# Issuing the adaLN weight and condition loads from GpSimd's queue in a two-layer diffusion backbone

## The chip, the cores and the metric

The kernel runs on one core of a Trainium2 chip. The metric is the device time of one execution in microseconds (us), the median over repeated executions. The profile is one execution taken by the hardware profiler.

## What is computed

Two layers of a diffusion backbone over 512 latent and 256 context tokens, width 1024, all in float32. Each layer is a half-step SwiGLU, a token mixer (differential attention in layer 0, windowed grouped-query attention in layer 1) and another half-step SwiGLU. Every sub-layer normalises its input and modulates it with shift, scale and gate vectors, which are products of the layer's adaLN matrix with SiLU of a condition:

```python
mod_l = (jax.nn.silu(c) @ ada_w[i] + ada_b[i])[:, None, :]      # 9 vectors of 1024 for latent tokens
mod_c = jax.nn.silu(c_ctx) @ ada_w[i] + ada_b[i]                # and for context tokens
sh1, sc1, g1, sh2, sc2, g2, sh3, sc3, g3 = jnp.split(mod_l, N_MOD, axis=-1)
def ffn_step(t, sh, sc, g, wi, wo):
    return t + 0.5 * g * swiglu(modulate(rms(t), sh, sc), wi, wo)
x = ffn_step(x, sh1, sc1, g1, pre_wi, pre_wo)
x = x + g2 * mixer(modulate(rms(x), sh2, sc2), ...)
x = ffn_step(x, sh3, sc3, g3, post_wi, post_wo)
```

## The kernel before, in words

TensorE (PE) multiplies everything as split float32: each operand is cut in a high part, made by ScalarE (L73), and a low part, made by VectorE (L74), and each product takes three matmuls. A weight slab of 512 KB is loaded into a tile `raw` (three buffers, L97) by a DMA that the sync engine SP issues; the tile is free again when VectorE has made the last low part from it (`wlo`, L74). The up products of a feed-forward use seven products where eight would be plain (L470), with sums of weights made by VectorE (L456 to L459) and sums of results (L479 to L507). The down products (L584) are added to the residual `x` by VectorE (L396).

The adaLN vectors 0 to 2 of layer 0 are made at the start (`vector_job`, L190, and `scale_job`, L205). All the others are made by `Halves`, beside the products of the feed-forwards before they are needed: one step is one load of 128 x 512 values of the adaLN matrix (`wh`, 256 KB, L247, three buffers) and one or two VectorE products with SiLU of the conditions (`ch`, L236 and L237) that sum along the row (L250). Eight steps fill `part`, and GpSimd adds it to the vector (L254); GpSimd also sets each vector to its bias ahead of that (`bias`, L227 and L229). `beside(3)` calls one step in each up block from the fifth on, `between(13)` 13 steps in the 16 tiles of a group of down products, and `oproj` two steps in a tile. There are 240 such loads and 16 of conditions: 80 steps in layer 0's first feed-forward, 16 in the attention's output product, 64 in layer 0's second feed-forward and 80 in layer 1's first.

The order on each engine's queue is set by a planner, when the program is built. It takes instructions as they become ready by its own estimate of their times, the earlier ones in the program's order first, and can move one ahead of others on its engine. `keep` (`tc.keep_in_program_order`) pins an instruction behind the one that the program last gave to the same engine; the loads L236 and L247 are kept, the slab loads L97 mostly are not. So before the change a load of `wh` stands on SP behind the slab load that the program issued last, and after it behind the last instruction that the program gave to GpSimd. Queues run in order: an instruction that waits for a free buffer holds what stands behind it.

GpSimd otherwise does little in the feed-forwards: sums of squares for the next normalisation in the last group of down products (L343), the power -1/2 (L300) and, in the attention, powers and rotary sums.

Of the kernel before, what the change touches and what calls it, by code (L numbers as in the profile page):

```python
# [17 lines left out]
P = 128  # L18
D = 1024
KC = D // P  # L20
# [22 lines left out]
def hybrid_backbone_kernel(ctx: ExitStack, tc: tile.TileContext, I, out):  # L43
    nc = tc.nc
# [25 lines left out]
    keep = tc.keep_in_program_order  # L70
# [143 lines left out]
    class Halves:  # L214
# [6 lines left out]
        def add(self, l, ms):  # L221
            def bias(m):
                md = const.tile([P, 2, KC], F32, name=f"mod{l}_{m}")
                mods[l][m] = md[:, 0], md[:, 1], md
                b = adab[:, l, m * KC:(m + 1) * KC].unsqueeze(1).broadcast_to([P, 2, KC])
                if m in (1, 4, 7):
                    nc.gpsimd.tensor_scalar_add(md, b, 1.0)  # L227
                else:
                    nc.gpsimd.tensor_copy(md, b)  # L229

            def silu(room, q):
                cs = []
                for nm in ("c", "c_ctx"):
                    pool, tag, bufs = (small, "ar", 3) if room[1] == "wh" else room
                    t = pool.tile([P, 512], F32, name="ch", tag=tag, bufs=bufs)
                    keep(nc.sync.dma_start(t, I[nm][q * 512:(q + 1) * 512].partition_broadcast(P)))  # L236
                    nc.scalar.activation(t, t, AF.Silu)  # L237
                    cs.append(t)
                self.c = cs

            def job(room, q, m, d):
                types = (0, 1) if l == 0 or m < 5 else (0,)
                if d == 0:
                    self.part = small.tile([P, 2, KC], F32, name="part", tag="part", bufs=2)
                pool, tag, bufs = room
                w = pool.tile([P, 512], F32, name="wh", tag=tag, bufs=bufs)
                keep(nc.sync.dma_start(w, I["ada_w"][l, m * KC + d, :, q * 512:(q + 1) * 512]))  # L247
                for ty in types:
                    o = w if ty == types[-1] else small.tile([P, 512], BF16, name="junkh", tag="tmp", bufs=4)
                    nc.vector.scalar_tensor_tensor(o, w, 1.0, self.c[ty], ALU.mult, ALU.mult,  # L250
                                                   accum_out=self.part[:, ty, d:d + 1])
                if d == KC - 1:
                    md, n = mods[l][m][2], len(types)
                    nc.gpsimd.tensor_add(md[:, :n], md[:, :n], self.part[:, :n])  # L254
                    if q == 1 and m in (2, 8):
                        nc.gpsimd.tensor_scalar_mul(md[:, :n], md[:, :n], 0.5)

            for q in range(2):
                for m in ms:
                    for d in range(KC):  # L260
                        def f(room, q=q, m=m, d=d):
                            if q == 0 and d == 0:
                                bias(m)
                            if m == ms[0] and d == 0:
                                silu(room, q)
                            job(room, q, m, d)
                        self.steps.append(f)
# [1041 lines left out]
```

## Time and profile before

| | us |
|---|---|
| median of 3 runs | 2820.3 (2819.34 to 2823.11) |
| the profiled execution's own time | 2823.49 |
| its span in the profile | 2821.3 |
| TensorE busy in the span | 2705.1 (96%) |
| VectorE busy | 2176.2 (77%) |
| ScalarE busy | 1205.7 (43%) |
| GpSimd busy | 339.3 (12%) |

Busy time of TensorE is that of its matmuls, which are pipelined. SP has no busy time in the profile, since instructions that issue DMAs are not counted; its waits are shown as those of SPq. In a wait, the engine on the left stood idle until the instruction on the right was done.

### The profile page before, as it was taken

What the parts mean: (1) busy time and instruction counts of PE and PEld (TensorE: products, weight loads), DVE (VectorE), ACT (ScalarE), POOL (GpSimd) and SP (SyncE); (2) the same over time, 40 slices, a digit from 0 to 9 for tenths busy, and PEclk for the clock granted to TensorE, in tenths of its full rate; (3) what the DMA queues carried; (4) which work ended last, traced back from release to release, by engine and by line L of the source; (5) the groups of instructions that cost most, each with busy time, mean ns of one, the idle gap of its engine ahead of it and who ended that gap; (6) DMA issues with size and microseconds to landing.
All of it is one profiled execution on the core that took longest, in us unless ns stands there. A gap on an engine that the chain in (4) does not pass through costs nothing. (4 is left out here: it accounts for less than half of the span.)

```text
span 2821.3 us, 47391 instructions
## 1 busy us (share of the span) xinstructions
PE 2705.1 (96%) x18028; PEld 2565.6 (91%) x18028; DVE 2176.2 (77%) x4703; ACT 1205.7 (43%) x2995; POOL 339.3 (12%) x464
## 2 busy tenths in 40 slices
PE   6899999999999899999999999999999999999999
PEld 4799998899999878999899989999999999999999
DVE  8788887876867768877787697777777766588887
ACT  4433332355656644333233352333235666444443
POOL 1000000034533421000000100000003421100000
PEclk9999999999999999999999999999999999999999
DMA  7234433321101142332333223433332101233232
GB/s 278 82 109 127 138 98 111 107 105 46 31 31 31 42 134 63 120 113 78 116 120 102 63 64 124 135 123 95 124 115 93 46 16 38 68 98 100 96 98 97
DMA packets 97555, 266.48 MB, mean 94 GB/s; under 512 B 12464, under 2 KB 16560, under 8 KB 97200
## 3 DMA queue, kind: packets, MB, share of 16 engines
q1 hardware_dynamic: 90816, 251.78, 27.6%
q10 hardware_dynamic: 6512, 11.68, 1.3%
q8 instruction: 142, 2.33, 0.3%
q14 instruction: 85, 0.70, 0.1%
HBM read 256.07 MB, written 7.34 MB: 93 GB/s over the span
## 5 line engine op out<-in xcount | busy, mean ns | idle before, releaser
L73 ACT CAST whi<-raw 128x512 fp32r<-128x512 f32 x548 | 336.1, 620 | 650.6 <-PE ps_dn L584 291.8
L584 PE MATMUL ps_dn<-ah,whi 128*128 128x256 f32 (+1 forms) x1456 | 464.9, 322 | 11.7 <-DVE x L396 9.5
L584 PE MATMUL ps_dn<-al,whi 128*128 128x256 f32 (+1 forms) x1456 | 462.2, 320 | 0.1
L584 PE MATMUL ps_dn<-ah,wlo 128*128 128x256 f32 (+1 forms) x1456 | 455.1, 319 | 1.1 <-DVE wlo L74 1.0
L74 DVE TENSOR_TENSOR wlo<-raw,whi 128x512 fp32r<-128x512 f32 x548 | 378.2, 695 | 65.5 <-ACT whi L73 49.9
L470 PE MATMUL ps_up<-h_h,whi 128*128 128x384 f32 (+1 forms) x1216 | 394.6, 325 | 8.3 <-DVE u L497 6.3
L470 PE MATMUL ps_up<-h_h,wlo 128*128 128x384 f32 (+1 forms) x1216 | 392.2, 324 | 0.7 <-DVE wlo L74 0.7
L470 PE MATMUL ps_up<-h_l,whi 128*128 128x384 f32 (+1 forms) x1216 | 392.5, 323 | 0.0
L396 DVE SCALAR_TENSOR_TENSOR x<-ps_dn,mod,x 128x256 f32<-128x256 f32 (+1 forms) x442 | 241.0, 556 | 126.6 <-PE ps_dn L584 103.0
L584 PEld LDWEIGHTS ps_dn<-ah,whi 128*128 128x128 f32 x1456 | 276.6, 191 | 35.8 <-ACT whi L73 8.5
L73 ACT CAST whi<-s 128x512 fp32r<-128x512 f32 x304 | 188.3, 620 | 266.6 <-PE ps_up L470 220.4
L584 PEld LDWEIGHTS ps_dn<-ah,wlo 128*128 128x128 f32 x1456 | 276.4, 191 | 21.8 <-DVE wlo L74 2.0
L584 PEld LDWEIGHTS ps_dn<-al,whi 128*128 128x128 f32 x1456 | 277.8, 191 | 19.6 <-DVE al L74 0.3
L470 PEld LDWEIGHTS ps_up<-h_h,whi 128*128 128x128 f32 x1216 | 229.0, 188 | 14.0 <-DVE u L497 8.9
L74 DVE TENSOR_TENSOR wlo<-s,whi 128x512 fp32r<-128x512 f32 x304 | 208.5, 687 | 31.4 <-ACT whi L73 27.7
L470 PEld LDWEIGHTS ps_up<-h_h,wlo 128*128 128x128 f32 x1216 | 228.3, 188 | 2.8 <-DVE wlo L74 2.3
L470 PEld LDWEIGHTS ps_up<-h_l,whi 128*128 128x128 f32 x1216 | 228.9, 188 | 0.5
L254 POOL TENSOR_TENSOR mod<-mod,part 128x16 f32<-128x16 f32 (+1 forms) x30 | 13.2, 439 | 1428.6 <-DVE wh L250 1428.6
L673 PE MATMUL ps_qkv<-whi,h_h 128*128 128x256 f32 x608 | 177.8, 292 | 3.2 <-DVE a L629 2.2
L250 DVE SCALAR_TENSOR_TENSOR wh<-wh,ch 128x512 f32<-128x512 f32 x240 | 163.4, 693 | 18.3 <-DMA wh<-in_ada_w 18.2
L673 PE MATMUL ps_qkv<-wlo,h_h 128*128 128x256 f32 x608 | 174.1, 286 | 0.7 <-DVE wlo L74 0.7
L673 PE MATMUL ps_qkv<-whi,h_l 128*128 128x256 f32 x608 | 173.6, 286 | 0.0
(236 smaller groups left out, 6536.5 us busy)
## 6 DMA issues: line engine op xcount, KB each, us to landing
wh<-in_ada_w SPq DMA_DIRECT2D x240, 256.0 KB, 3.8
raw<-in_pre_wi SPq DMA_DIRECT2D x88, 512.0 KB, 3.5
raw<-in_post_wi SPq DMA_DIRECT2D x88, 512.0 KB, 3.5
raw<-in_pre_wo SPq DMA_DIRECT2D x44, 512.0 KB, 3.6
raw<-in_post_wo SPq DMA_DIRECT2D x44, 512.0 KB, 3.6
araw<-in_ada_w SPq DMA_DIRECT2D x16, 512.0 KB, 4.4
raw<-in_a_w_qk SPq DMA_DIRECT2D x16, 512.0 KB, 3.5
araw<-in_ada_s SPq DMA_DIRECT2D x8, 512.0 KB, 10.0
```

The costliest lines, as they stand in the source:

```text
L73: nc.scalar.copy(hi, src)
L74: nc.vector.tensor_sub(lo, src, hi.bitcast(F32))
L250: nc.vector.scalar_tensor_tensor(o, w, 1.0, self.c[ty], ALU.mult, ALU.mult, accum_out=self.part[:, ty, d:d + 1])
L254: nc.gpsimd.tensor_add(md[:, :n], md[:, :n], self.part[:, :n])
L396: nc.vector.scalar_tensor_tensor(x[:, d, s0:s0 + n], ps, gate[ty][:, d:d + 1], x[:, d, s0:s0 + n], ALU.mult, ALU.add)
L470: nc.tensor.matmul(ps, ww, z[:, k, :n], start=first and k == 0 and i == 0, stop=k == 3 and i == 2, skip_group_check=True)
L584: nc.tensor.matmul(ps, wv, a[:, s0:s0 + n], start=fi == 0 and k == 0, stop=fi == nf - 1 and k == 2)
L673: nc.tensor.matmul(ps, h[:, k, bt], w, start=n == 0, stop=n == 23)
```

## The change

The loads of the condition halves and of the adaLN weight halves are issued by GpSimd instead of SP. Their `keep` stays, and so pins them on the other queue. Nothing else is edited.

```diff
@@ def silu(room, q):
                     t = pool.tile([P, 512], F32, name="ch", tag=tag, bufs=bufs)
-                    keep(nc.sync.dma_start(t, I[nm][q * 512:(q + 1) * 512].partition_broadcast(P)))
+                    keep(nc.gpsimd.dma_start(t, I[nm][q * 512:(q + 1) * 512].partition_broadcast(P)))
                     nc.scalar.activation(t, t, AF.Silu)
@@ def job(room, q, m, d):
                 w = pool.tile([P, 512], F32, name="wh", tag=tag, bufs=bufs)
-                keep(nc.sync.dma_start(w, I["ada_w"][l, m * KC + d, :, q * 512:(q + 1) * 512]))
+                keep(nc.gpsimd.dma_start(w, I["ada_w"][l, m * KC + d, :, q * 512:(q + 1) * 512]))
```

## Rows read from the trace of the kernel before

**Rows 1.** The page: span, and busy time and count of two engines.

```profile
span 2821.3 us, 47391 instructions
PE 2705.1 (96%) x18028; PEld 2565.6 (91%) x18028; DVE 2176.2 (77%) x4703; ACT 1205.7 (43%) x2995; POOL 339.3 (12%) x464
```

**Rows 2.** Stretches: length, busy PE, PEld, DVE, ACT, POOL (instructions), clock, DMA share, GB/s.

```profile
70.00:80.00 10.00, 3.46 (x19) 2.70 (x17) 10.00 (x29) 2.17 (x5) 0.00 (x0) 0.90 0.00 0
...
330.00:564.00 234.00, 225.69 (x1283) 210.59 (x1282) 191.17 (x423) 73.53 (x131) 2.48 (x6) 1.00 0.35 113
...
1130.00:1550.00 420.00, 412.55 (x2334) 390.81 (x2333) 338.03 (x713) 142.50 (x261) 4.11 (x8) 0.99 0.33 108
1690.00:2100.00 410.00, 408.43 (x2316) 386.81 (x2315) 318.00 (x651) 138.53 (x252) 4.91 (x11) 1.00 0.38 122
```

**Rows 3.** Waits, 121 to 564 us: who, for whom; us in total, times, longest.

```profile
DVE junkh L250 <- DMA wh<-in_ada_w: 6.7, 7, 1.8
PE ps_up L470 <- DVE u L497: 3.2, 1, 3.2
PE ps_dn L584 <- DVE x L396: 3.2, 1, 3.2
```

**Rows 4.** Waits, 1090 to 1560 us.

```profile
DVE junkh L250 <- DMA wh<-in_ada_w: 7.3, 7, 1.9
PE ps_dn L584 <- DVE x L396: 5.4, 3, 3.2
```

**Rows 5.** Waits, 1690 to 2110 us.

```profile
DVE wh L250 <- DMA wh<-in_ada_w: 18.2, 18, 2.3
...
PE ps_up L470 <- DVE u L491: 0.4, 1, 0.4
```

**Rows 6.** Waits of PE, 990 to 1130 us (the attention's output product).

```profile
PE ps_dn L750 <- DVE wlo L74: 2.7, 1, 2.7
```

**Rows 7.** DVE in order of time, 330 to 346 us: start, length [idle before].

```profile
334.31 0.69 DVE L250 SCALAR_TENSOR_TENSOR junkh<-wh,ch 128x512 bf16<-128x512 f32 x1 [1.76 <-DMA wh<-in_ada_w]
...
340.71 0.69 DVE L250 SCALAR_TENSOR_TENSOR junkh<-wh,ch 128x512 bf16<-128x512 f32 x1 [1.10 <-DMA wh<-in_ada_w]
```

**Rows 8.** Waits of SP's queue over the whole span.

```profile
SPq L97 <- DVE wlo L74: 1912.3, 261, 46.4
SPq L247 <- DVE wh L250: 130.1, 108, 5.3
```

**Rows 9.** SP's queue in order of time, 260 to 330 us.

```profile
262.35 14.60 SPq L97 DMA_DIRECT2D raw<-in_pre_wi  x2
277.00 1.19 SPq L247 DMA_DIRECT2D wh<-in_ada_w  x1
```

**Rows 10.** SP's queue in order of time, 0 to 135 us.

```profile
120.43 0.42 SPq L236 DMA_DIRECT2D ch<-in_c  x1
```

**Rows 11.** The tile `wh`: durations in ns (min/median/max), starts; DMA to landing.

```profile
L247 SPq DMA_DIRECT2D wh<-in_ada_w x240: 327/422/1867, 121.4 to 2088.2; - x120
L250 DVE SCALAR_TENSOR_TENSOR wh<-wh,ch x240: 675/685/1219, 128.9 to 2092.5; 128x512 f32<-128x512 f32 x120
...
DMA to landing us min/median/max: 2.5/3.8/6.3
```

**Rows 12.** GpSimd in order of time, 0 to 135 us.

```profile
16.44 0.20 POOL L229 COPY mod<-adab 128x16 f32<-128x16 f32 x1 [16.01 <-DMA adab<-in_ada_b]
...
21.69 1.04 POOL L300 TENSOR_TENSOR r<-v,neghalf 128x4 f32<-128x4 f32 x1
22.69 0.19 POOL L229 COPY mod<-adab 128x16 f32<-128x16 f32 x1
26.09 1.21 POOL L300 TENSOR_TENSOR r<-v,neghalf 128x2 f32<-128x2 f32 x1 [3.20 <-DVE v L298]
```

**Rows 13.** The line L229: durations in ns (min/median/max), first and last start.

```profile
L229 POOL COPY mod<-adab x10: 191/266/1198, 16.4 to 22.7; 128x16 f32<-128x16 f32 x10
```

**Rows 14.** DVE in order of time, 0 to 135 us.

```profile
22.76 0.69 DVE L305 TENSOR_TENSOR dg<-ident,r 128x512 f32<-128x512 f32 x1 [1.79 <-POOL r L300]
```

**Rows 15.** Groups on GpSimd, 121 to 564 us: busy, mean ns, idle before.

```profile
L254 POOL TENSOR_TENSOR mod<-mod,part 128x16 f32<-128x16 f32 x10 | 4.3, 432 | 510.4 <-DVE wh L250 510.4
```

## The prediction, as it was put on record

> **What bounds the kernel now.** I read the page's busy times first. TensorE is busy 2705.1 of 2821.3 us [rows 1], so all that any edit of loads can win is the 116 us in which it isn't. Then the stretches in which the moved loads run, three feed-forwards: there it is busy 225.7 of 234, 412.6 of 420 and 408.4 of 410 us [rows 2]. Then who made TensorE wait in them, and whether that one had itself waited for a moved load. In layer 0's first feed-forward VectorE waited 6.7 us for `wh`, and TensorE lost 3.2 us to the residual sum L396 and 3.2 us to L497 [rows 3]; in the second one VectorE waited 7.3 us, and TensorE lost 5.4 us to L396 [rows 4]; in layer 1's, VectorE waited most, 18.2 us, and TensorE lost 0.4 us [rows 5]. Of these stalls the one to L396 in rows 3 has its cause in sight: 2.86 us of waits for `wh` on VectorE [rows 7], shortly ahead of it on the same queue. The reader is to see that late `wh` loads cost VectorE some 32 us, and that at most about 10 of them reach TensorE.
>
> **The change, part by part.** The sum is made against the profiled execution, 2823.5 us (a span of 2821.3 and 2.2 around it); it lies 3.2 us above the median of the runs, and I subtract that at the end.
>
> *SP loses 256 issues.* An issue takes 0.42 us [rows 11], but SP's time is waiting: 1912 us for `raw` buffers, and only 130 us, in 108 waits, at a `wh` load [rows 8]. A slab load behind such a wait comes at most some 1.2 us sooner, with a buffer that is its true limit. Worth 0.
>
> *GpSimd gains 256 issues.* In a feed-forward it works 4.3 of 443 us on L254 [rows 15], so the issues have cover there; what stands behind a load that waits for its tile is L254, for which only later stages wait. The duration of an issue on GpSimd isn't in this trace. From below it is SP's 0.42 us [rows 11], from above the 1.21 us of a small power [rows 12]; I take 1.04 us, the other power, since it is an instruction of the same queue at the place where it counts. 0 in the feed-forwards.
>
> *The start.* Here there is no cover. The planner takes the bias copies L229 as early as it can: all ten, those of layer 1 too, run from 16.4 to 22.7 us [rows 13], though the program has most of them hundreds of us later. The first two `ch` loads will be pinned behind the first of these copies and nothing else; their tile is free from the beginning, so I expect them at about 17 us instead of 120.4 [rows 10]. The power that the first normalisation needs waits on that queue behind the copies until 21.69 us [rows 12], and VectorE waits 1.79 us for it [rows 14]. Two issues ahead of it make it 2 x 1.04 = 2.1 us later, and VectorE, which soon after has no idle time left (10.00 of 10 us busy, with TensorE at 3.5, [rows 2]), passes that on. +2.1 us; ends 0 (the planner puts them behind the power) and 2 x 1.21 = 2.4 us. A gain is excluded, as nothing leaves that queue.
>
> *The pace.* Before, a `wh` load waits behind the slab load ahead of it: two slab loads hold SP from 262.35 to 276.95 us, and the next `wh` goes out at 277.00 [rows 9]. After, it is pinned only behind the biases, long done, or, in a vector's second half, behind the L254 of the vector before. So it goes out as soon as its tile is free, and its sums fill VectorE's idle time from the start of a stage, rather than come in bursts of 13 steps. What this can win is the stalls after late loads: 3.2 us of L396 in rows 3, 5.4 in rows 4, and 2.7 in the output product [rows 6], 11.3 in all; from below 0. I take the two long ones, 3.2 + 3.2 = -6.4 us: the first has late loads ahead of it, the second (the longest in rows 4) I take to have the same cause, and the short ones look like plain crowding of VectorE.
>
> *The landing.* A `wh` lands 3.8 us after issue now, at most 6.3 [rows 11]. How late it lands from GpSimd isn't shown: 0 to 2.5 us later (6.3 - 3.8); I take 1.0, about one GpSimd instruction ahead of the transfer. VectorE waits for `wh` in 7 + 7 + 18 = 32 cases, and TensorE loses 3.2 + 3.2 + 0.4 = 6.8 us (the longest ones) for 32.2 us of those waits, a share of 0.21 [rows 3 to 5]. With deeper prefetch I expect half as many waits at the landing, those after each L254 among them: 16 x 1.0 x 0.21 = +3.4 us; ends 0 and the second rival below.
>
> Sum: 2.1 - 6.4 + 3.4 = -0.9 us, 2822.6 for the profiled execution, 2819.4 for the median: 2819 us, which a measurement of this kernel can't tell from no change (it takes about 0.2%, 5.6 us).
>
> One rule bears on the first step. Rows 8 show a queue that waits for buffers and not for its own issue time. The Trainium skill ("DMA: Bandwidth & Descriptors", section "Issuing engines are not separate DMA queues") says that DMAs from any engine run on the same 16 DMA engines, and that another issuer saves only the sequencer's time. By that rule alone the sum would be 0; it leaves out the order of the queue that the load moves to, which is what my terms come from.
>
> **The rivals.**
>
> *The new pace clears all the crowding (faster).* Every sum is done ahead of need, and no load is waited for: -11.3, with 0 to +2.1 at the start, about -10 us: 2810. For it: in the last stretch VectorE is less full (318 of 410 us, against 338 of 420) and its waits no longer reach TensorE [rows 2, 5]. Against it: the sums will keep VectorE full for longer, and a queue without slack passes on every slip.
>
> *Descriptors held up (slower).* GpSimd's work is held while VectorE runs an instruction with large operands: L229 takes 266 ns as a rule and 1198 at most [rows 13]. If an issue is held so too, `wh` lands up to 2.5 us late, the planner's places for the sums are too early, and each third load is waited for, not each seventh: 80 x 1.0 x 0.21 = +17 us, 2837; with 2.5 us, 80 x 2.5 x 0.21 = +42 us, 2862. It decides once `wh` takes over about 5 us to land and VectorE's waits for it pass some 80 us. Against it: in a feed-forward L254 takes 432 ns in the mean beside a VectorE that is as full [rows 15].
> The skill ("SBUF — State Buffer", section "SBUF: two separate sides") says that such loads starve while VectorE copies or casts in a two-port mode, and "Who interferes with whom" there exempts sums of two tensors. By the first the time would be this rival's; by the second it would not come about. No row of before has such a load.
>
> *It does nothing (same).* The planner keeps the sums where they stand, since VectorE's order is set by its other work; loads come earlier and wait in their tiles: 2820.
>
> **How the numbers follow.** Forecast (2819, terms cancelling) 0.35; nothing happens 0.13; all crowding clears 0.28; descriptors held up 0.24. Faster by over 0.2% (below 2814.7): 0.29, the faster rival and a little of the forecast's own spread. Slower (above 2825.9): 0.25. Within: 0.46. The range starts at 2808 (the largest gains, 2820.3 - 11.3, and 1 us of the runs' spread) and reaches up to 2838, the slower rival at its middle price; beyond lie the held-up loads at their full price.
>
> **What would show it.** Right: `ch` loads at some 17 us on GpSimd's queue and the power after 23 us; `wh` loads ahead of the slab loads beside them; VectorE's waits for `wh` below 32 us; no TensorE stall of 3 us near 343 and 1370 us. Wrong: a landing over 5 us, or new waits of TensorE on VectorE early in each feed-forward, where the sums now crowd; or an order on VectorE in all later stages that differs so much that the stalls of the attention, which no step here touches, move by several us.

## The result, and the profile after

The changed kernel takes 2869.8 us in the median of 4 runs (2865.42 to 2875.09), the kernel before 2821.5 us beside it: a ratio of 1.0166, 95% interval [1.0153, 1.0179]. It is slower by 48 us, where 2819 us and no measurable change were forecast, and the time lies outside the range.

The profiled execution of the changed kernel took 2865.4 us. Its page gives the span, the busy times and, in the last line, the issues of `wh` (count, size, median us from issue to landing); it answers to [rows 1].

```profile
span 2863.6 us, 47501 instructions
...
PE 2712.5 (95%) x18028; PEld 2572.9 (90%) x18028; DVE 2179.2 (76%) x4703; ACT 1205.4 (42%) x2995; POOL 476.8 (17%) x720
...
wh<-in_ada_w POOLq DMA_DIRECT2D x240, 256.0 KB, 3.2
```

The span has grown by 42.3 us, of which TensorE's busy time is only 7.4 (2712.5 less 2705.1): the other 35 us are idle time of TensorE. VectorE does the same work (2179.2 against 2176.2 us). So the work itself hardly became dearer; something now stands in TensorE's way. The same stretches as in [rows 2], after (length, then busy PE, PEld, DVE, ACT, POOL, then clock, DMA share, GB/s):

```profile
1130.00:1550.00 420.00, 396.68 (x2244) 374.90 (x2243) 331.79 (x701) 137.36 (x252) 36.00 (x68) 0.98 0.31 100
...
1690.00:2100.00 410.00, 394.17 (x2222) 371.36 (x2222) 308.65 (x627) 134.69 (x247) 45.18 (x87) 0.99 0.35 113
```

TensorE is idle for 23.3 and 15.8 us there, where it was idle for 7.4 and 1.6. To see which part of the program pays, I cut both traces at the first product of each stage (for a feed-forward, L537 and then L470; for the attention, L673 or L686; for its output, L750). Length of each stage in us, and TensorE's idle time in it:

```
stage                                   before         after        after - before
start                                118.7 / 34.2   117.7 / 33.9       -1.0
layer 0, first feed-forward          480.7 / 11.7   487.7 / 15.8       +7.0
layer 0, attention                   403.9 / 24.7   398.5 / 21.6       -5.4
layer 0, output product               84.2 /  7.3    84.1 /  8.4       -0.1
layer 0, second ff, blocks of L537    55.4 /  1.8    59.5 /  2.7       +4.1
layer 0, second ff, from L470 on     481.5 / 10.1   497.6 / 26.0      +16.1
layer 1, first ff, blocks of L537     60.4 /  3.2    65.4 /  6.1       +5.0
layer 1, first ff, from L470 on      473.3 /  4.3   490.9 / 18.5      +17.6
layer 1, attention                   238.6 /  5.6   238.7 /  5.8       +0.1
rest                                 424.7 / 10.0   423.6 /  9.0       -1.1
```

The three feed-forwards with sums beside them give 49.8 us; the other stages give 7.5 back. Two profiled executions of one and the same kernel (the first experiment below and its repeat) differ by up to 4.2 us in a stage, so the 7.0 of layer 0's first feed-forward and the -5.4 of its attention lie little above the scatter; what is clear of it are layer 0's second feed-forward and layer 1's first. Where the sums went is seen by asking for VectorE's busy time of L250 alone, stretch by stretch, at the start and the end of layer 0's second feed-forward. Before (length, busy us of these instructions and their count, clock, DMA share, GB/s):

```profile
1088.00:1143.00 55.00, 0.00 (x0) 0.97 0.13 42
1143.00:1163.00 20.00, 4.17 (x13) 1.00 0.55 171
1163.00:1203.00 40.00, 11.99 (x36) 1.00 0.34 112
...
1400.00:1640.00 240.00, 32.27 (x96) 0.99 0.29 93
```

After, the same stretches:

```profile
1088.00:1143.00 55.00, 10.11 (x30) 0.91 0.32 103
1143.00:1163.00 20.00, 8.05 (x23) 0.73 0.20 62
1163.00:1203.00 40.00, 19.18 (x59) 0.92 0.53 169
...
1400.00:1640.00 240.00, 0.00 (x0) 1.00 0.20 67
```

Up to 1163 us VectorE now has 18.2 us of sums, where it had 4.2: 14.0 us more. And there was no room for them. All engines in the first of these stretches, before (PE, PEld, DVE, ACT, POOL):

```profile
1088.00:1143.00 55.00, 53.18 (x338) 48.63 (x338) 52.55 (x109) 28.43 (x62) 0.75 (x1) 0.97 0.13 42
```

VectorE was busy for 52.55 of 55 us without a single sum in it. The 14 us more come out at TensorE as one stall. The longest waits after, whole span (who, for whom; us in total, times, longest):

```profile
PE ps_up L470 <- ACT whi L73: 22.2, 6, 14.6
```

VectorE's queue in order of time, at the end of that stall (start, length, idle before; no idle time stands in these lines), then ScalarE's:

```profile
1155.36 0.68 DVE L456 TENSOR_TENSOR s<-raw 128x512 f32<-128x512 f32 x1
1155.96 0.68 DVE L250 SCALAR_TENSOR_TENSOR junkh<-wh,ch 128x512 bf16<-128x512 f32 x1
...
1159.54 0.68 DVE L457 TENSOR_TENSOR s<-s,raw 128x512 f32<-128x512 f32 x1
1160.15 0.68 DVE L250 SCALAR_TENSOR_TENSOR wh<-wh,ch 128x512 f32<-128x512 f32 x1
...
1161.84 0.68 DVE L458 TENSOR_TENSOR s<-raw 128x512 f32<-128x512 f32 x1
1162.44 0.68 DVE L250 SCALAR_TENSOR_TENSOR junkh<-wh,ch 128x512 bf16<-128x512 f32 x1
...
1163.05 0.68 DVE L459 TENSOR_TENSOR s<-raw,s 128x512 f32<-128x512 f32 x1
```

```profile
1163.77 0.62 ACT L73 CAST whi<-s 128x512 fp32r<-128x512 f32 x1 [5.15 <-DVE s L459]
```

This is the whole chain: TensorE needs the high part `whi` of a sum of weights `s`, ScalarE waits 5.15 us for `s`, and the four instructions that make it (L456 to L459) stand on VectorE with sums of adaLN halves between them. VectorE has no idle time during the stall, so it is not waiting for a load there. TensorE's clock pays as well. The same 20 us before and after:

```profile
1150.00:1170.00 20.00, 19.92 (x114) 19.53 (x113) 18.98 (x46) 8.87 (x17) 0.00 (x0) 1.00 0.50 167
```

```profile
1150.00:1170.00 20.00, 5.56 (x20) 5.55 (x21) 19.81 (x50) 5.48 (x11) 4.48 (x9) 0.57 0.36 110
```

With TensorE busy for 5.56 us instead of 19.92, the granted clock of the stretch is 0.57 instead of 1.00, near the lower of its two levels (1.2 of 2.4 GHz); over the whole execution it is 0.981 against 0.988.

The two other feed-forwards differ. Layer 1's first has the same wait once more, with 6.6 us (waits of TensorE after, 1640 to 2180 us):

```profile
PE ps_up L470 <- ACT whi L73: 7.0, 2, 6.6
```

Layer 0's first has no such stall; just ahead of its first L470 VectorE had room. All engines from 98 to 118 us, before and after, where 8.37 us of sums came in:

```profile
98.00:118.00 20.00, 20.00 (x120) 17.57 (x119) 8.74 (x16) 5.94 (x12) 0.00 (x0) 1.00 0.10 36
98.00:118.00 20.00, 20.00 (x123) 17.77 (x122) 18.84 (x47) 7.58 (x16) 4.29 (x8) 1.00 0.39 129
```

TensorE is busy for all of that stretch in both.

Why the sums came to the start of layer 0's second feed-forward is on GpSimd's queue (start, length, idle before):

```profile
1092.61 0.62 POOL L236 DMA_DIRECT2D ch<-in_c  x1 [3.49 <-ACT h_h L380]
1103.23 0.54 POOL L236 DMA_DIRECT2D ch<-in_c_ctx  x1 [10.00 <-ACT h_h L380]
1103.76 1.60 POOL L247 DMA_DIRECT2D wh<-in_ada_w  x3
```

and on SP's before:

```profile
1144.89 0.42 SPq L236 DMA_DIRECT2D ch<-in_c  x1
1145.36 0.42 SPq L236 DMA_DIRECT2D ch<-in_c_ctx  x1
1145.83 0.43 SPq L247 DMA_DIRECT2D wh<-in_ada_w  x1
```

The first weight load of this feed-forward goes out 42 us earlier. Over the whole span the loads ran from 121.4 to 2088.2 us [rows 11]; now they are all out by 1863.4. VectorE's idle time in front of its sums until a load landed (us, times), before:

```profile
  DMA wh<-in_ada_w: 34.6, 37
```

The same after, with the issues and the landing of `wh`:

```profile
L247 POOL DMA_DIRECT2D wh<-in_ada_w x240: 536/538/652, 77.9 to 1863.4; - x120
...
  DMA wh<-in_ada_w: 24.9, 29
...
DMA to landing us min/median/max: 2.7/3.2/9.1
```

### The profile page after: what moved, and what is told of

Same layout as the page of the kernel before. It is cut to its first block, busy times and chain, and to the rows that moved or that the text cites. A ratio compares the mean times of both kernels' runs of the same rounds, so it can differ in the third digit from the quotient of the medians.

```text
span 2863.6 us, 47501 instructions
## 1 busy us (share of the span) xinstructions
PE 2712.5 (95%) x18028; PEld 2572.9 (90%) x18028; DVE 2179.2 (76%) x4703; ACT 1205.4 (42%) x2995; POOL 476.8 (17%) x720
## 5 line engine op out<-in xcount | busy, mean ns | idle before, releaser
L470 PE MATMUL ps_up<-h_h,whi 128*128 128x384 f32 (+1 forms) x1216 | 398.7, 328 | 28.9 <-ACT whi L73 21.4
L470 PE MATMUL ps_up<-h_h,wlo 128*128 128x384 f32 (+1 forms) x1216 | 394.4, 326 | 3.5 <-DVE wlo L74 3.5
L470 PE MATMUL ps_up<-h_l,whi 128*128 128x384 f32 (+1 forms) x1216 | 396.0, 326 | 0.0
L396 DVE SCALAR_TENSOR_TENSOR x<-ps_dn,mod,x 128x256 f32<-128x256 f32 (+1 forms) x442 | 241.6, 555 | 120.9 <-PE ps_dn L584 100.6
L470 PEld LDWEIGHTS ps_up<-h_h,whi 128*128 128x128 f32 x1216 | 232.0, 191 | 34.6 <-ACT whi L73 22.3
L247 POOL DMA_DIRECT2D wh<-in_ada_w x240 | 130.3, 544 | 696.8 <-DVE wh L250 614.3
L470 PEld LDWEIGHTS ps_up<-h_h,wlo 128*128 128x128 f32 x1216 | 231.1, 190 | 5.2 <-DVE wlo L74 5.2
L470 PEld LDWEIGHTS ps_up<-h_l,whi 128*128 128x128 f32 x1216 | 232.0, 191 | 0.4
L343 POOL TENSOR_TENSOR ar<-ar,sq 128x256 f32<-128x256 f32 x84 | 69.6, 834 | 711.7 <-ACT sq L341 709.6
L673 PE MATMUL ps_qkv<-whi,h_h 128*128 128x256 f32 x608 | 177.2, 291 | 3.4 <-DVE a L629 2.4
L673 PE MATMUL ps_qkv<-wlo,h_h 128*128 128x256 f32 x608 | 173.6, 286 | 0.8 <-DVE wlo L74 0.7
L673 PE MATMUL ps_qkv<-whi,h_l 128*128 128x256 f32 x608 | 173.1, 285 | 0.0
```

The lines of the kernel that those rows point to most:

```text
L247: keep(nc.gpsimd.dma_start(w, I["ada_w"][l, m * KC + d, :, q * 512:(q + 1) * 512]))
L343: add(self.acc[p], self.acc[p], sq)
L396: nc.vector.scalar_tensor_tensor(x[:, d, s0:s0 + n], ps, gate[ty][:, d:d + 1], x[:, d, s0:s0 + n], ALU.mult, ALU.add)
L470: nc.tensor.matmul(ps, ww, z[:, k, :n], start=first and k == 0 and i == 0, stop=k == 3 and i == 2, skip_group_check=True)
L673: nc.tensor.matmul(ps, h[:, k, bt], w, start=n == 0, stop=n == 23)
```

## The experiments

Two theories stood at first. *Pace*: the `keep` on SP held each load behind the slab load that the program had given last, and that was the only thing that spread the sums over a feed-forward; on GpSimd nothing spreads them. *Queue*: GpSimd's own issues, or loads from its queue beside those of SP, cost the time. Each verdict below is against the kernel before, run on the same chip.

**Same queue, old pace.** The edit against the changed kernel: the loads stay on GpSimd; an edge that the planner alone sees (no semaphore) puts each behind the slab load that SP got last.

```diff
+    def beside_sp(ins):
+        prev = next(i for i in reversed(nc.cur_bb.bb.instructions) if i.engine == mybir.EngineType.SP)
+        return tc.add_manual_dep(ins.ins, prev.name, mybir.DependencyInfo(mybir.DependencyClass.NoSync, ...
-                keep(nc.gpsimd.dma_start(w, ...))
+                beside_sp(keep(nc.gpsimd.dma_start(w, ...)))      # and so for ch
```

> The moved loads stay on GpSimd, but the planner must place each of them (and each condition load) behind the slab load that the program last gave to SP, as before the change; the edge is one of the planner's order alone, nothing waits for it on the chip. Theory A (the order: freed from SP, the planner draws the row sums into the first blocks of each feed-forward, where VectorE is full, and TensorE stalls): back to 2820, between 2808 and 2828; no stall of TensorE over 4 us after the start, where the changed kernel has 14.65 and 6.6 us. Theory B (the queue: an issue from GpSimd costs by itself, through its landing, VectorE's waits for it, or shared ports): stays at 2860 to 2870.

2814.5 us against 2822.1, ratio 0.9972 [0.9962, 0.9983]. The whole loss is gone, with all 256 issues on GpSimd at the same price:

```profile
L247 POOL DMA_DIRECT2D wh<-in_ada_w x240: 536/538/590, 77.2 to 2077.0; - x120
```

The queue theory falls. Run again, for the small gain itself:

> The paced form (all 256 loads from GpSimd's queue, each planned behind the slab load that the program last gave to SP) a second time, in more rounds, to settle whether it beats the kernel before: 2810 to 2818 us, ratio 0.995 to 0.999. If the 0.28% of the first time were chance of that chip, the ratio would be within 0.1% of 1.

2813.6 us against 2824.7, 0.9965 [0.9952, 0.9977]: the gain of 0.3% is real.

**Old queue, new pace.** The mirror: issue from SP, as before, but without `keep` on the two loads.

```diff
-                keep(nc.sync.dma_start(w, ...))
+                nc.sync.dma_start(w, ...)      # and so for ch
```

> The kernel before with the loads on SP, but without the pin on the condition and weight-half loads, so that the planner may take them ahead of the slab loads. Theory A: slow like the changed kernel, 2850 to 2880, with the sums early in each feed-forward and a stall of TensorE of several us at its start. Theory B: 2820 within 8 us, as no load is issued from GpSimd.

2874.7 us against 2822.1, 1.0181 [1.0157, 1.0205]: the loss without one issue on GpSimd. Tile `wh`, and TensorE's longest waits from 1090 to 1640 us:

```profile
L247 SPq DMA_DIRECT2D wh<-in_ada_w x240: 327/328/1201, 77.4 to 1838.8; - x120
```

```profile
PE ps_up L470 <- ACT whi L73: 17.0, 5, 14.6
```

Even the stall is the same, 14.6 us. With the run before this shows the cause from both sides.

**Which loads.** The 16 `ch` loads alone on GpSimd; `wh` stays on SP with its `keep`:

```diff
-                    keep(nc.sync.dma_start(t, ...))
+                    keep(nc.gpsimd.dma_start(t, ...))
```

> Only the 16 condition loads go to GpSimd; the 240 weight-half loads stay pinned on SP. Theory A: the sums keep their pace, 2820 within 8 us, and at most 2 us more at the start for two issues ahead of the first normalisation's power. Theory B: 16 of 256 issues, so 1/16 of the loss of 48 us, 2823. If the early condition loads by themselves do harm (ScalarE's SiLU of them waits in order), 2835 or more.

2826.9 us against 2822.1, 1.0015 [1.0004, 1.0027]. Either theory allows that (2820 within 8, or 2823); what it excludes is that the early `ch` loads do the harm by themselves. The 240 `wh` loads alone; `ch` stays on SP:

```diff
-                keep(nc.sync.dma_start(w, ...))
+                keep(nc.gpsimd.dma_start(w, ...))
```

> Only the 240 wh loads go to GpSimd's queue; the 16 ch loads stay pinned behind a slab load on SP's. The first sums of each feed-forward can't start before the first ch load of that feed-forward, which keeps its old place. Pace (order): about the kernel that gates only the ch loads, 2838 us (2830 to 2848), without the 14 us stall at the start of layer 0's second feed-forward, since the sums still crowd once they may start. Density alone being harmless would give 2815 to 2822; the queue itself being the cost (240 of 256 loads are on it) 2870.

2836.7 us against 2824.7, 1.0042 [1.0026, 1.0058]. And all on GpSimd, with only the `ch` loads planned behind SP's slab loads, as in the first experiment (the edit against the kernel before):

```diff
-                    keep(nc.sync.dma_start(t, ...))
+                    beside_sp(keep(nc.gpsimd.dma_start(t, ...)))
-                keep(nc.sync.dma_start(w, ...))
+                keep(nc.gpsimd.dma_start(w, ...))
```

> As changed, all loads on GpSimd, but the planner must place the condition loads behind the slab load that the program last gave to SP, so that no step starts before the fifth block of its feed-forward; from there the weight halves are free. Theory A in the form that the harm is the early start (the sums meet the sums of weights and inputs of blocks two to four): 2820 to 2832, the stalls of 14.65 and 6.6 us gone. Theory A in the form that the harm is the density (sums without pace at any place): 2845 to 2865, with stalls in the blocks from the fifth on. Theory B: 2860 to 2870.

2838.6 us against 2822.1, 1.0062 [1.0041, 1.0082]: between the two forecasts, 2820 to 2832 if the early start does the harm and 2845 to 2865 if the density does. The last two agree; both hold the first sums of a feed-forward at their old place and leave the others free. In layer 0's second feed-forward that is enough: from the first L470 on it takes 483.1 and 481.5 us, as before the change (481.5), and has no stall of over 5 us. The 12.0 and 16.5 us that stay in the medians lie in the other two: layer 0's first (489.0 and 488.0 against 480.7) and layer 1's first (487.1 and 485.7 against 473.3); other stages give some of it back. In layer 1's the start is as empty of sums as before, but from 1725 to 1765 us VectorE has 14.0 and 14.3 us of them, where it had 1.4; TensorE's waits, up to 2.6 us, lie there and in the second half of the stage. So part of the loss comes with the early start, and a part with what lies behind it. Close spacing is not enough for a loss: from 1183 to 1223 us, in layer 0's second feed-forward, VectorE of the first of these two kernels has 17.05 us of sums where it had 2.77, is all but full, and TensorE loses nothing (busy for 39.88 of 40 us before the change):

```profile
1183.00:1223.00 40.00, 39.82 (x229) 36.71 (x228) 38.93 (x93) 9.93 (x18) 7.02 (x15) 1.00 0.44 139
```

Why it costs TensorE time in layer 1's first feed-forward and not here, these runs do not show.

**Half the sums.** Each sum runs over 256 of 512 columns (half of the adaLN products is left out); every load stays. Once from the changed kernel, once from the kernel before, as a control.

```diff
-                    nc.vector.scalar_tensor_tensor(o, w, 1.0, self.c[ty], ALU.mult, ALU.mult,
+                    nc.vector.scalar_tensor_tensor(o[:, :256], w[:, :256], 1.0, self.c[ty][:, :256], ...
```

> The changed kernel, with each sum taken over 256 of 512 columns: half of VectorE's work on the sums (about 0.69 to 0.4 us each) is left out, every load and issue is kept. If the loss is the sums crowding VectorE at the start of a feed-forward, it shrinks to less than half: against the kernel before with the same half sums +5 to +20 us instead of +48, and the stall at the start of layer 0's second feed-forward falls from 14.7 us to below 6. If the loss comes from the loads themselves (issue from GpSimd, transfers beside slab loads) it stays at about +48 us against that control.

> Control: the kernel before, with each sum taken over 256 of 512 columns (half of VectorE's work on the sums left out). VectorE's waits for its sums reach TensorE little in the kernel before, so 2805 to 2822 us, 0 to 15 us below the kernel before. A larger gain would say that the sums cost TensorE time already in the old order.

2839.0 and 2840.6 us, against 2824.7. The two are within 2 us of each other, where the pace theory wanted 5 to 20 us and the queue theory 48. But the control missed: with less work it is slower than the kernel before, 1.0059 [1.0042, 1.0076], so this pair does not tell the theories apart. Its trace suggests why it is no control: VectorE, done sooner with each sum, now stands at the landing of the next load. Before that was 34.6 us in 37 waits; here:

```profile
  DMA wh<-in_ada_w: 115.8, 69
```

That these waits make it slower is not shown; a form further below has 81.2 us of them at no price. The stall at the start of layer 0's second feed-forward was 10.7 us in the halved changed kernel, not below 6 as expected; the shorter sums are pulled ahead as well.

**One tile instead of three for `wh`**, on the changed kernel, to thin the sums out by their buffers:

```diff
-                self((i + 1) * n // 16 - i * n // 16, (seven.pool, "wh", 3))
+                self((i + 1) * n // 16 - i * n // 16, (seven.pool, "wh", 1))      # and so in the up blocks
```

> The changed kernel with one tile for the weight halves in place of three: order and issuer stay, but a step can start only when the one before is done, about 0.5 of issue, 3.2 of landing and 1.5 of sums, 5.2 us a step, so the sums take at most 29% of VectorE at the start of a feed-forward. If their density does the harm: 2820 to 2848 us, the 14.7 us stall at the start of layer 0's second feed-forward below 5 us. If the early start alone does it, or VectorE then waits at the landing of each load, 2855 us or more.

2869.6 us against 2822.3, 1.0169 [1.0154, 1.0184]: nothing won. The long stall did shrink, from 14.6 to 4.7 us, but VectorE now waits for more than half of the loads to land (134 of 240):

```profile
DVE junkh L250 <- DMA wh<-in_ada_w: 138.2, 93, 3.9
DVE wh L250 <- DMA wh<-in_ada_w: 64.5, 41, 4.2
```

The second of the two ways named in advance for a loss is there; the first, the early start, is not excluded, since the sums still start early. So this run does not isolate the density.

**Pace by the products.** If the place of the sums is what counts, the best place is the one where the program calls each step, in an up block or a tile of down products. So each load is planned behind the product that TensorE got last (`EngineType.PE` in place of `EngineType.SP` in the helper above), once from GpSimd with its `keep` and once from SP without it.

```diff
-                keep(nc.sync.dma_start(w, ...))
+                beside_pe(keep(nc.gpsimd.dma_start(w, ...)))      # the first kernel, and so for ch
+                beside_pe(nc.sync.dma_start(w, ...))              # the second
```

> All 256 loads from GpSimd's queue, each planned behind the product that the program last gave to TensorE, so that the steps stand where the program calls them, one or two in an up block. If the cost is where the sums stand on VectorE, not which queue issues or whether SP's slab loads set the pace, this comes out like the form paced by SP: 2808 to 2822 us, no TensorE stall over 5 us in a feed-forward. If the slab loads' pace is needed as such, 2835 or more.

> The same pace by TensorE's products, with the loads issued from SP's queue. If the queue is worth only what the first paced form won (about 0.3%), this lies 0 to 10 us above the form on GpSimd: 2810 to 2832 us. A gap of over 20 us between the two would say that the queue matters after all (slab loads held behind loads that wait for their tile).

From GpSimd 2801.4 us, 0.9929 [0.9914, 0.9944]; from SP 2791.1 us (2788.66 to 2793.98), 0.9891 [0.9876, 0.9905], both against 2822.3. Both beat both kernels of this case, the second by 31 and 79 us. Both also lie below their forecasts (2808 to 2822, and 2810 to 2832), and the one from SP was expected to be the slower. The sums of the second in the stretches shown above (this form is at the first L470 of that feed-forward at 1128.3 us, 14.6 us sooner than the kernel before), and VectorE's waits for its loads:

```profile
1088.00:1143.00 55.00, 0.00 (x0) 1.00 0.18 58
1143.00:1163.00 20.00, 0.69 (x2) 1.00 0.47 145
1163.00:1203.00 40.00, 14.22 (x42) 1.00 0.36 119
...
1400.00:1640.00 240.00, 32.87 (x96) 0.99 0.29 93
```

```profile
DVE junkh L250 <- DMA wh<-in_ada_w: 5.8, 10, 1.5
DVE wh L250 <- DMA wh<-in_ada_w: 2.6, 7, 0.6
```

The full start of the stage is now free of sums altogether (0.69 us up to 1163 us, against 4.2 before and 18.2 after), and VectorE waits 8.4 us for landings, against 34.6 before. TensorE is idle for 5.8, 3.4 and 2.7 us in the three feed-forwards from the first L470 on, against 11.7, 10.1 and 4.3 before.

**A third queue.** The edit of the change with ScalarE's queue in place of GpSimd's, `keep` and all: the loads are pinned behind ScalarE's last instruction, of which a feed-forward is full.

```diff
-                keep(nc.sync.dma_start(w, ...))
+                keep(nc.scalar.dma_start(w, ...))      # and so for ch
```

> The edit of the change with ScalarE's queue in place of GpSimd's, the keep as it is: each load is pinned behind the last instruction that the program gave to ScalarE, which has work all through a feed-forward. If the pace decides, the loads keep a pace of the program's and the loss of 48 us doesn't come: 2812 to 2835 us, with the ScalarE issues (256 of some 0.5 us, 2 ends) as the only new cost. If leaving SP's queue is what costs, 2860 or more.

2822.3 us against 2822.3, 1.0005 [0.9995, 1.0014]. Leaving SP costs nothing when the new queue has a pace of its own. In this trace VectorE waits for landings longer than before the change, at no visible price:

```profile
  DMA wh<-in_ada_w: 81.2, 67
```

All forms with the full computation side by side, medians in us:

```
pace of the loads                      from GpSimd         from SP
free                                   2869.8 (change)     2874.7
behind SP's last slab load             2814.5, 2813.6      2822 (before)
behind TensorE's last product          2801.4              2791.1
```

From row to row of this table the time moves by 12 to 56 us, from column to column by 5 to 10, and there not even in one direction. The pace is the cause. (The runs were made on more than one chip; the kernel before took 2821.5 to 2824.7 us beside each of them.)

## Why the prediction was wrong

*The pace* is the step that failed. What happens to the loads was seen rightly: a load would no longer wait behind a slab load and would go out as soon as its tile was free. Its sign was wrong. The step says that the sums "fill VectorE's idle time from the start of a stage, rather than come in bursts of 13 steps", priced -6.4 us, and from the bad side only "from below 0", nothing. The only figures for VectorE's idle time in a feed-forward that the prediction reads are means over whole stretches, such as 338.03 of 420 us [rows 2]; the step puts that idle time where the sums would go. At the start of layer 0's second feed-forward there was hardly any, 52.55 of 55 us, and the row that shows it could have been read in the trace of before. With it the stall there could have been foreseen: 14.0 us more of sums up to 1163 us, on an engine without a gap, for which TensorE waits by way of L456 to L459 and `whi`, 14.6 us long. Over the three feed-forwards the term was +49.8 us instead of -6.4: 20.2 in layer 0's second, 22.6 in layer 1's first and 7.0 in layer 0's first. For the last two the stall at the start explains only a part, 6.6 us in layer 1's and nothing in layer 0's; what makes up the rest stays open. The text did name the sign of this failure ("new waits of TensorE on VectorE early in each feed-forward, where the sums now crowd"), but gave it no price, no place among the rivals and no chance. Most of the signs that it named for being right came true as well (`ch` early, VectorE's waits for `wh` at 24.9 us, no stall of 3 us at L396): they watch the loads, and not the work that the sums push back.

The gain that the step counted on was partly there: no wait for L396 in layer 0's first feed-forward is over 0.8 us now, where one was 3.2 [rows 3]. It was far too small. The 11.3 us that I put as the most were no upper end for what a pace can win: behind TensorE's products it won 31 us, of which TensorE's idle time in the three feed-forwards from the first L470 on gives 14.2; how much of it are stalls after late loads no run shows.

*SP loses 256 issues*: predicted at 0; no run shows it apart from what GpSimd gains. With the pace of SP's loads the whole move won 0.3%, with that of TensorE's products it lost 10 us.

*GpSimd gains 256 issues*: an issue takes 538 ns, nearer to the lower end (0.42) than to the 1.04 us taken. In the changed kernel no issue of a `wh` took longer than 652 ns beside a VectorE that is busy for 76% of the span; the longest of a `ch` took 0.76 us, at the start.

*The start*: half right. The `ch` loads came to the place foreseen, and the power behind them later:

```profile
15.82 0.76 POOL L236 DMA_DIRECT2D ch<-in_c  x1
16.59 0.56 POOL L236 DMA_DIRECT2D ch<-in_c_ctx  x1
...
22.38 1.05 POOL L300 TENSOR_TENSOR r<-v,neghalf 128x4 f32<-128x4 f32 x1
```

The power starts 0.69 us later than in [rows 12], not 2.1, and the start stage is 1.0 us shorter, not longer, within the spread of the forms (116.3 to 119.3 us). The term was 0, inside its ends.

*The landing*: wrong in sign and without weight. From GpSimd a `wh` lands 3.2 us after issue in the median, against 3.8 before [rows 11], and VectorE waits for it 24.9 us in 29 cases, against 34.6 in 37. Nor does the queue set the landing: with the same free pace it is 3.0 us from SP, and paced by TensorE's products 3.3 from GpSimd and 3.7 from SP. The share of 0.21 by which I let landing waits reach TensorE is not supported either: from ScalarE they rose by 46.6 us (81.2 less 34.6), which would have been +10 us by that share, and the time is the same, though the pace differs too.

*The rivals.* Descriptors held up: false by its own conditions (landing over 5 us, waits over 80 us), though its time, 2862 at the full price, lies near the result; a right size for a wrong reason. The section of the Trainium skill that was weighed there ("SBUF — State Buffer", "SBUF: two separate sides") speaks of loads starved beside two-port modes; the `wh` issues of 536 to 652 ns show none of that. No run here puts it to the test, though: beside the loads VectorE runs sums, products and low parts, and its only large copies read results of TensorE. All crowding clears: the opposite came about. It does nothing: false.

*The rule beside the first step* (the Trainium skill, "DMA: Bandwidth & Descriptors", "Issuing engines are not separate DMA queues") is not contradicted: at equal pace the issuer moved the time by 5 to 10 us, and not in one direction. What it leaves out, the order that a queue gives to its loads, was worth 48 us, and that the order was where to look the prediction did say.

What stays open: why the planner's own estimate has room for the sums at the full start of a stage; and why, behind TensorE's products, SP is 10 us better than GpSimd (7.8 of it in layer 0's first feed-forward), while behind slab loads it is 8 us worse. In that pair the `keep` differs too, and no run separates the two.

## What to carry to other kernels

A queue is not only a place to issue from: an in-order queue, or a pin on it, can be what spaces background work out, and moving a load to an empty queue takes that spacing away. Before freeing such work, read how full its engine is at the moment when the work would now start, in a window of a few tens of us, not the mean of the stage, and what that engine owes the busiest one at that moment; and if the spacing is wanted, ask for it by itself, tied to the product beside which the work belongs, which here was worth 1.1%.

## What the runs showed of the hardware

The issue of a 256 KB load took 538 ns on GpSimd in the median, 328 to 423 on SP by the form of the kernel, and 334 on ScalarE. The landing of the same load was 3.0 to 3.9 us in the median in the forms with all three tiles and whole sums, and moved as much with the pace on one queue (3.0 to 3.9 from SP) as between queues. TensorE's busy time is not a constant of its work: the same 18028 matmuls took 2712.5 us with the stalls (clock 0.981), 2705.1 before (0.988) and 2692.0 in the best form (0.989); between the last two the clock is all but the same, so it is not the whole reason. VectorE full to 38.93 of 40 us left TensorE busy for 39.82 of them (only `wh` on GpSimd, from 1183 us), and VectorE full to 19.81 of 20 us left it busy for 5.56 (the changed kernel, from 1150 us).
